# Input gain moved from the projection weights to the rows of x, weight blocks split in pieces of 1024 columns, two pools widened

## The chip, the cores and the metric

The kernel runs as one program on one core of a Trainium2 chip. The metric is the device time of one execution in microseconds (us), the median of several runs. Five engines are meant below: PE (matrix products, with its weight loads shown as PEld), DVE, ACT, POOL, and SP, which here issues every DMA. Each engine takes its instructions in order; semaphores tie the engines together.

## What is computed

Two layers (DEPTH = 2) over 2048 tokens of 1024 float32 features. In each:

```python
h = rmsnorm(x, pre_g)                       # y * pre_g, over the 1024 features
P = h @ W_in                                # 1024 x 2816, columns: u, v, g_A, q, k, v_B, g_B
y_A = u * (W_s @ layernorm(v) + b) * silu(g_A)     # in chunks of 128 tokens, 8 groups of 64
y_B = attention(rope(rmsnorm(q)), rope(rmsnorm(k)), v_B) * silu(g_B)   # 8 query heads, 2 kv heads
x = x + rmsnorm(concat(y_A, y_B) @ W_out, post_g)
```

`pre_g` is a vector of 1024 numbers for each layer. It multiplies the columns of the normalised x, and so can equally multiply the rows of `W_in`.

## The kernel before

**Stages.** A layer is a projection stage and an attention stage. The trace has them at about 0 to 633 us and 633 to 1380 us for layer 0, then to 2011 and 2750 us for layer 1. The projection goes in two halves of two groups; a group (GRP) is 512 tokens.

**Normalised x.** `hT_jobs` gives the jobs of a group. `prep` loads a row tile `x_t` (128 tokens x 1024), lets ACT square it, computes the reciprocal root on DVE with eight tiny operations, and scales it on DVE (L294, two operations of 512 columns) by the row's factor and a constant. `trans` turns it with PE and splits it into a high and a low part, `hT`. The first two groups of layer 1 are scaled in the attention of layer 0 instead (`scale`, L982, tile `x_r`), stored to `h_d`, and read back as `x_h`.

**Weights.** `W_in` is worked off in blocks of 1024 x 256, held as 128 x 8 x 256: one `w_raw` (1 MB, 8 KB a partition), from which `split_w` makes `w_hi` (rounded, ACT, L263) and `w_lo` (the rest, DVE, L264). A product is three passes over them, high x high, high x low, low x high. In `split_w` both operations also multiply by the gain `g_pre`, a pointer to one number per partition; since the gain differs between the eight slices of 128 rows, there are 8 + 8 operations of 256 columns a block. A half has eleven blocks, called here in their order K (keys and values), Q, Q2, VA, VA2, GB, GB2, and four of gates, G0 to G3. The block after the one in use is loaded and split while PE works on the one in use.

**Buffers.** `w_raw`, `w_hi`, `w_lo` and some tiles of the attention share pool `wp`, six buffers of 8 KB a partition. Small work tiles (`fa`, `fb`, `fc`, `fh`, `fl`, `x_h`) share pool `fp`, ten buffers of 2 KB. A tile is given a buffer in program order, and its first writer waits until the last reader of the buffer's former tile is done.

**Order.** Instructions written with `PE`, `ACT`, `DVE`, `POOL` in capitals keep their program order. Those written with `nc.` are placed among them by a scheduler that goes by the tiles' dependences and when buffers become free. So a change of buffers also changes the order on the engines. `bg` is a list of small jobs (transposes, spatial weights) of which the projection does one or two between its passes. `at(k, f)` does the same at step k of the attention. Layer 1's `begin` (block K) is called there, three steps after the end of layer 0's attention.

Of the kernel before, what the change touches and what calls it, by code (L numbers as in the profile page):

```python
# [9 lines left out]
F32 = mybir.dt.float32  # L10
# [3 lines left out]
AF = mybir.ActivationFunctionType  # L14
ALU = mybir.AluOpType
# [4 lines left out]
P = 128  # L20
D = 1024
ND = D // P
GRP = 512
# [6 lines left out]
C_U, C_VA, C_GA, C_Q, C_K, C_GB = 0, 512, 1024, 1536, 2048, 2304  # L30
# [4 lines left out]
NORM_SCALE = -8192.0 / D ** 0.5  # L35
# [3 lines left out]
def encoder(ctx: ExitStack, tc, x, w_in, w_out, pre_g, post_g, ln_a_g, ln_a_b,  # L39
            spatial_w, spatial_b, q_norm_g, k_norm_g, rope, out):  # L40
    nc = tc.nc
# [6 lines left out]

    const = ctx.enter_context(tc.tile_pool(name="const", bufs=1))
    big = ctx.enter_context(tc.tile_pool(name="big", bufs=6))  # L50
    wp = ctx.enter_context(tc.tile_pool(name="wp", bufs=6))
    fp = ctx.enter_context(tc.tile_pool(name="fp", bufs=10))
    rowp = ctx.enter_context(tc.tile_pool(name="rowp", bufs=5))
    lay = ctx.enter_context(tc.tile_pool(name="lay", bufs=1))
    small = ctx.enter_context(tc.tile_pool(name="small", bufs=2))
# [3 lines left out]
    def big_t(shape, name, dt=F32R):  # L59
        return big.tile(shape, dt, name=name, tag="big")  # L60

    def w_t(shape, name, dt=F32R):
        return wp.tile(shape, dt, name=name, tag="w")

    def f_t(name, n=GRP, dt=F32):
        return fp.tile([P, n], dt, name=name, tag="f")

    def row_t(name, shape=(P, D), dt=F32):
        return rowp.tile(list(shape), dt, name=name, tag="row")

    def ps_t(name):
        return psum.tile([P, GRP], F32, name=name, tag="ps", bufs=7)

    class Pinned:


        def __init__(self, engine):
            self.engine = engine
# [8 lines left out]
    PE, ACT, DVE, POOL = Pinned(nc.tensor), Pinned(nc.scalar), Pinned(nc.vector), Pinned(nc.gpsimd)  # L87
# [23 lines left out]
    def x_src(l, t):  # L111
        return x[0, t * P:(t + 1) * P, :] if l == 0 else xn_d[l - 1][t]
# [15 lines left out]
    def rsqrt_row_steps(ss, z, tag, v):  # L128


        m = small.tile([P, 1], F32, name="rs_m", tag=f"rs_m{tag}")
        t = small.tile([P, 1], F32, name="rs_t", tag=f"rs_t{tag}")
        steps = [lambda: v.tensor_scalar(m, ss[:, 0:1], ss[:, 1:2], D * EPS, ALU.add, ALU.add),
                 lambda: v.tensor_scalar(z.bitcast(I32), m.bitcast(I32), -0.5, RSQRT_MAGIC, ALU.mult, ALU.add)]
        for c in (-3.0, -12.0, -768.0):
            steps += [lambda: v.tensor_scalar(t, z, z, m, ALU.mult, ALU.mult),
                      lambda c=c: v.tensor_scalar(z, t, c, z, ALU.add, ALU.mult)]
        return steps
# [36 lines left out]
    class Project:  # L175
        def __init__(self, l):
            self.l = l
            self.stores = []

        def begin(self):  # L180

            self.g_pre = lay.tile([P, ND], F32, name="g_pre", bufs=2)
            raw = self.load_w([C_K])
            nc.sync.dma_start(self.g_pre, pre_g[self.l].rearrange("(t p) -> p t", p=P))
            self.w_kv = self.split_w(raw)

        def gains(self):
            l = self.l
# [65 lines left out]
                                  w_in[self.l, :, c:c + n].rearrange("(d p) e -> p d e", p=P))  # L254
            return raw

        def split_w(self, raw):

            hi = w_t([P, ND, WB], "w_hi")
            lo = w_t([P, ND, WB], "w_lo")  # L260
            for d in range(ND):
                g = self.g_pre[:, d:d + 1]
                nc.scalar.activation(hi[:, d], raw[:, d], AF.Copy, scale=g)  # L263
                nc.vector.scalar_tensor_tensor(lo[:, d], raw[:, d], g, hi.bitcast(F32)[:, d],  # L264
                                               ALU.mult, ALU.subtract)
            return hi, lo

        def hT_jobs(self, g, tail=False):

            hT = [big_t([P, 2, ND // 2, GRP], "hT") for _ in range(2)]  # L270
            xs = [None] * TPG
            act, dve = (ACT, DVE) if tail else (nc.scalar, nc.vector)

            def prep(j):
                def f():
                    done = self.l > 0 and g < HN
                    src = h_d[g * TPG + j] if done else x_src(self.l, g * TPG + j)
                    if done:
                        xs[j] = xt = [f_t("x_h") for _ in range(2)]
                        for i in range(2):  # L280
                            nc.sync.dma_start(xt[i], src[:, i * GRP:(i + 1) * GRP])
                        return
                    row = row_t("x_t")
                    xs[j] = xt = [row[:, 0:GRP], row[:, GRP:D]]
                    nc.sync.dma_start(row, src)
                    junk = ps_t("sq")
                    parts = small.tile([P, 2], F32, name="ss_x", bufs=4)
                    for i in range(2):
                        nc.scalar.activation(junk, xt[i], AF.Square, accum_out=parts[:, i:i + 1])
                    z = small.tile([P, 1], F32, name="rs_x", bufs=4)  # L290
                    for f in rsqrt_row_steps(parts, z, "x", nc.vector):
                        f()
                    for i in range(2):
                        nc.vector.tensor_scalar(xt[i], xt[i], z, 1.0 / NORM_SCALE, ALU.mult, ALU.mult)  # L294
                return f

            def trans(j, q):
                def f():
                    ps = ps_t("pt").rearrange("p (d t) -> p d t", d=4)
                    for d in range(4):  # L300
                        PE.transpose(ps[:, d, :], xs[j][q][:, d * P:(d + 1) * P], ident)
                    sl = slice(j * P, (j + 1) * P)
                    act.copy(hT[q][:, 0, :, sl], ps)
                    dve.tensor_tensor(hT[q][:, 1, :, sl], ps, hT[q].bitcast(F32)[:, 0, :, sl], ALU.subtract)  # L304
                return f
            return hT, [prep(j) for j in range(TPG)], [trans(j, q) for j in range(TPG) for q in range(2)]
# [316 lines left out]
    def attend(l, kv, nxt):  # L623
# [25 lines left out]
        def at(k, f):  # L649
            later.setdefault(k, []).append(f)  # L650
# [298 lines left out]
        def post_steps(s, t, last=False):  # L949
            z = small.tile([P, 1], F32, name="rs_o", bufs=4)  # L950

            def gain(i):
                sl = slice(i * WB, (i + 1) * WB)
                return lambda: POOL.tensor_tensor(s.o[:, sl], s.o[:, sl], g_post[:, sl], ALU.mult)

            def add(hf):
                def f():
                    sl = slice(hf * GRP, (hf + 1) * GRP)
                    DVE.scalar_tensor_tensor(s.o[:, sl], s.o[:, sl], z, s.x[:, sl], ALU.mult, ALU.add)
                    if last and nxt is None:  # L960
                        nc.sync.dma_start(x_dst(l, t)[:, sl], s.o[:, sl])
                return f

            steps = ([gain(i) for i in range(D // WB)] if last else []) + rsqrt_row_steps(s.ss, z, "o", DVE) + [add(0), add(1)]
            def store():
                nc.sync.dma_start(x_dst(l, t), s.o)

            if not last:
                steps.append(store)
            elif nxt is not None:  # L970
                nxt.stores.append(store)
            if nxt is not None and t < HN * TPG:
                ss = small.tile([P, 2], F32, name="ss_o", bufs=4)
                zh = small.tile([P, 1], F32, name="rs_o", bufs=4)

                def square(hf):
                    sl = slice(hf * GRP, (hf + 1) * GRP)
                    return lambda: ACT.activation(s.x[:, sl], s.o[:, sl], AF.Square, accum_out=ss[:, hf:hf + 1])

                def scale(hf):  # L980
                    sl = slice(hf * GRP, (hf + 1) * GRP)
                    return lambda: DVE.tensor_scalar(s.x[:, sl], s.o[:, sl], zh, 1.0 / NORM_SCALE,  # L982
                                                     ALU.mult, ALU.mult)

                steps += [square(0), square(1)] + rsqrt_row_steps(ss, zh, "o", DVE) + [scale(0), scale(1)]
                steps.append(lambda: nc.sync.dma_start(h_d[t], s.x))
            return steps
# [91 lines left out]

        load, last = last_steps()  # L1080
        if nxt is not None:
            at(end + 3, nxt.begin)
        at(total - LAST_0 - 7, load)
        at(total - LAST_0, begin_last)
        for k in range(end + 4):
            if k < total:
                u, i = k // NT, k % NT
                s = state[u]
# [25 lines left out]
            if 0 <= kb < total:  # L1114
                u, i = kb // NT, kb % NT
                s = state[u]
# [5 lines left out]
            if 0 <= kb < total:  # L1122
                u, i = kb // NT, kb % NT
                s = state[u]
# [25 lines left out]
        n = 0  # L1150
# [74 lines left out]
```

## Time and profile before

| | us |
|---|---|
| median of 3 runs (lowest, highest) | 2789.05 (2789.04, 2790.42) |
| the profiled execution | 2785.91 |
| its span in the trace | 2784.1 |
| mean granted clock of PE | 0.994 |
| PE busy | 2681.2 (96%) |
| DVE busy | 1928.6 (69%) |
| ACT busy | 1576.0 (57%) |
| POOL busy | 1279.2 (46%) |
| 352 copies to `w_hi` on ACT, sum | 150.7 |

Busy time is the time in which an engine has an instruction under way; the span runs from the first instruction to the last. About 1.8 us of an execution lie outside the span. The rows of the trace name a line, an engine, an operation, and the tile written and those read.

### The profile page before, as it was taken

How to read it: one execution, taken by the hardware profiler on the slowest of the kernel's cores; microseconds unless marked ns; L12 is line 12 of the kernel's file. 1: busy time of each engine (PE TensorE's matmuls, PEld its weight loads, DVE VectorE, ACT ScalarE, POOL GpSimd, SP SyncE). 2: the span in 40 equal slices, each digit the busy share in tenths (PEclk: the TensorE clock that was granted, in tenths of full speed). 3: DMA queues.
4: the chain of work that ended last, by engine and by line, in shares of the span. 5: the costliest groups of instructions: out<-in, count | busy, mean ns of one | idle time of the engine just before them, and what ended most of it. 6: DMA issues, size and time to landing. Idle time of an engine off the chain costs nothing.

```text
span 2784.1 us, 49014 instructions
## 1 busy us (share of the span) xinstructions
PE 2681.2 (96%) x18230; PEld 1781.7 (64%) x18230; DVE 1928.6 (69%) x4056; ACT 1576.0 (57%) x3263; POOL 1279.2 (46%) x1080
## 2 busy tenths in 40 slices
PE   7999999999999999999999999999999999999997
PEld 7898889764444444444598989897644454444444
DVE  7873797886666766666497638888766666666664
ACT  5322432127887787777642225322288877777774
POOL 1210121007786676767532001210187867767765
PEclk9999999999999999999999999999999999999999
DMA  4433422322222222223344334223222222221313
GB/s 125 142 102 119 144 76 75 115 70 85 87 70 75 85 91 82 81 72 95 126 149 135 118 111 147 73 88 107 84 76 72 74 78 69 75 84 47 104 59 130
DMA packets 277107, 264.31 MB, mean 95 GB/s; under 512 B 21250, under 2 KB 235394, under 8 KB 276868
## 3 DMA queue, kind: packets, MB, share of 16 engines
q1 hardware_dynamic: 276868, 261.18, 29.8%
q8 instruction: 143, 2.34, 0.4%
q14 instruction: 96, 0.79, 0.1%
HBM read 176.05 MB, written 85.07 MB: 94 GB/s over the span
## 4 chain that ended last, share of the span: by engine, by line
PE 75%; DVE 14%; ACT 5%; issue 2%; DMA 2%; SPq 0%; POOL 0%; DVEq 0%; ACTq 0%; POOLq 0%
PE pp L84 26%; PE sp L84 14%; PE pout L84 11%; PE po L84 11%; PE pmax L84 7%; PE sums L84 4%; PE pt L84 2%; DVE w_lo L264 2%; DVE fc L357 2%; ACT p_parts L84 2%; ACT p_f L84 2%; DVE mx L677 1%; DVE fb L442 1%; DMA w_raw<-in_w_in_dram 1%; DVE o_t L84 1%
## 5 line engine op out<-in xcount | busy, mean ns | idle before, releaser
L84 POOL TENSOR_TENSOR p_parts<-p_f,p_parts 128x512 f16<-128x512 f32 x872 | 1032.9, 1203 | 404.2 <-ACT p_f L84 301.7
L84 ACT ACTIVATE p_parts<-sp 128x512 f16<-128x512 f32 x1024 | 628.8, 614 | 293.8 <-PE sp L84 287.3
L84 DVE TENSOR_REDUCE mx<-pmax 128x1 f32<-128x512 f32 x768 | 512.9, 681 | 210.4 <-PE pmax L84 208.5
L84 PE MATMUL pout<-wo,y_t 128*128 128x512 f32 x1488 | 656.1, 505 | 0.6 <-ACT p_f L84 0.3
L84 PE MATMUL po<-p_parts,v_st 128*32 128x512 f16 (+1 forms) x3072 | 638.0, 383 | 0.2
L84 ACT ACTIVATE p_f<-sp 128x512 f32<-128x512 f32 x1024 | 630.0, 615 | 0.0
L84 PE MATMUL pp<-w_hi,hT 128*128 128x256 f32 x3584 | 502.7, 289 | 14.8 <-DVE hT L304 10.1
L84 PEld LDWEIGHTS pp<-w_hi,hT 128*128 128x128 f32 x3584 | 462.2, 194 | 24.6 <-DVE hT L304 10.7
L84 PE MATMUL pmax<-k_t,q_m 128*128 128x512 f16 x1024 | 389.3, 382 | 10.7 <-DVE mx L677 3.3
L84 PE MATMUL sp<-q_st,k_t 128*128 128x512 f16 x1024 | 389.5, 380 | 7.3 <-DVE mx L84 4.6
L84 PEld LDWEIGHTS <-v_st 128*32 128x32 f16 (+1 forms) x3072 | 193.2, 96 | 309.2 <-issue 252.1
L84 PE MATMUL sp<-q,k_t 66*128 66x512 f16 x1024 | 390.4, 381 | 0.0
L84 PEld LDWEIGHTS pout<-wo,y_t 128*128 128x128 f32 x1488 | 280.8, 190 | 128.3 <-issue 9.2
L84 PEld LDWEIGHTS <-k_t 128*128 128x128 f16 (+1 forms) x2048 | 191.4, 99 | 186.6 <-issue 73.2
L462 POOL TENSOR_TENSOR fl<-fa,fh 128x512 fp32r<-128x512 f32 x32 | 42.1, 1317 | 518.6 <-ACT fh L461 430.4
L84 PE MATMUL pp<-hT,w_hi 128*128 128x512 f32 x1024 | 271.7, 413 | 0.0
L84 PE MATMUL pp<-w_lo,hT 128*128 128x256 f32 x1792 | 264.0, 288 | 5.7 <-DVE w_lo L264 5.5
L263 ACT ACTIVATE w_hi<-w_raw,g_pre 128x256 fp32r<-128x256 f32 x352 | 150.7, 499 | 171.8 <-DMA w_raw<-in_w_in_dram 111.1
L84 PE MATMUL sums<-p_parts,one_h 128*32 128x512 f16 x2048 | 242.1, 380 | 0.0
L84 PEld LDWEIGHTS pp<-w_lo,hT 128*128 128x128 f32 x1792 | 233.8, 192 | 10.8 <-DVE w_lo L264 9.3
L84 PEld LDWEIGHTS pp<-hT,w_hi 128*128 128x128 f32 x1024 | 193.2, 189 | 35.4
L677 DVE TENSOR_REDUCE mx<-pmax 128x1 f32<-128x512 f32 x256 | 173.0, 686 | 37.0 <-PE pmax L84 35.3
(160 smaller groups left out, 2839.9 us busy)
## 6 DMA issues: line engine op xcount, KB each, us to landing
w_raw<-in_w_in_dram SPq DMA_DIRECT2D x28, 1024.0 KB
y_t<-y_d SPq DMA_DIRECT2D x56, 512.0 KB
w_raw<-in_w_in_dram SPq DMA_DIRECT2D x32, 512.0 KB
x_t<-in_x_dram SPq DMA_DIRECT2D x16, 512.0 KB
z_d<-fb SPq DMA_DIRECT2D x32, 256.0 KB
gb_d<-fa SPq DMA_DIRECT2D x32, 256.0 KB
fb<-z_d SPq DMA_DIRECT2D x32, 256.0 KB
y_d<-fh SPq DMA_DIRECT2D x32, 256.0 KB
```

Source lines behind the costliest of these rows:

```text
L84: return tc.keep_in_program_order(call(*args, **kw))
L263: nc.scalar.activation(hi[:, d], raw[:, d], AF.Copy, scale=g)
L264: nc.vector.scalar_tensor_tensor(lo[:, d], raw[:, d], g, hi.bitcast(F32)[:, d], ALU.mult, ALU.subtract)
L357: nc.vector.tensor_tensor(t2[:, :, :, lo:lo + 16], qn[:, :, :, hi:hi + 16], tbi[:, :, 1:2, lo:lo + 16].broadcast_to([P, 2, n, 16]), ALU.mult)
L442: nc.vector.scalar_tensor_tensor(s.zt[r, c, :], pz[r, h * P:(h + 1) * P], self.lng[r, c:c + 1], self.zbias[r, c, :], ALU.mult, ALU.add)
L462: nc.gpsimd.tensor_tensor(lo, th, hi.bitcast(F32), ALU.subtract)
L677: dve.tensor_reduce(s.mx[:, j, c:c + 1], ps, AX.X, ALU.max)
```

## The change

The gain is no longer applied in `split_w`. A new function `norm_row` loads `pre_g` of a layer as one row, copied to all 128 partitions (`g_row`, 128 x 1024, 512 KB written), and ACT multiplies it by the constant. The scale of `x_t` and that of `x_r` then multiply by the row's factor and by `g_row`. `split_w` makes plain copies and plain subtractions of four slices, 1024 columns; for the K block in `begin`, of two. The load of `g_pre` is gone. `wp` gets a seventh buffer, `fp` twelve instead of ten.

```diff
-    wp = ctx.enter_context(tc.tile_pool(name="wp", bufs=6))
-    fp = ctx.enter_context(tc.tile_pool(name="fp", bufs=10))
+    wp = ctx.enter_context(tc.tile_pool(name="wp", bufs=7))
+    fp = ctx.enter_context(tc.tile_pool(name="fp", bufs=12))
...
+        def norm_row(self):
+            self.g_row = lay.tile([P, D], F32, name="g_row")
+            nc.sync.dma_start(self.g_row, pre_g[self.l].partition_broadcast(P))
+            nc.scalar.mul(self.g_row, self.g_row, 1.0 / NORM_SCALE)
...
         def begin(self):
-            self.g_pre = lay.tile([P, ND], F32, name="g_pre", bufs=2)
-            raw = self.load_w([C_K])
-            nc.sync.dma_start(self.g_pre, pre_g[self.l].rearrange("(t p) -> p t", p=P))
-            self.w_kv = self.split_w(raw)
+            self.w_kv = self.split_w(self.load_w([C_K]), 2)
...
-        def split_w(self, raw):
+        def split_w(self, raw, n=4):
             hi = w_t([P, ND, WB], "w_hi")
             lo = w_t([P, ND, WB], "w_lo")
-            for d in range(ND):
-                g = self.g_pre[:, d:d + 1]
-                nc.scalar.activation(hi[:, d], raw[:, d], AF.Copy, scale=g)
-                nc.vector.scalar_tensor_tensor(lo[:, d], raw[:, d], g, hi.bitcast(F32)[:, d],
-                                               ALU.mult, ALU.subtract)
+            for d in range(0, ND, n):
+                sl = slice(d, d + n)
+                nc.scalar.copy(hi[:, sl], raw[:, sl])
+                nc.vector.tensor_tensor(lo[:, sl], raw[:, sl], hi.bitcast(F32)[:, sl], ALU.subtract)
...
                     nc.sync.dma_start(row, src)
+                    if self.g_row is None:
+                        self.norm_row()
...
-                        nc.vector.tensor_scalar(xt[i], xt[i], z, 1.0 / NORM_SCALE, ALU.mult, ALU.mult)
+                        nc.vector.scalar_tensor_tensor(xt[i], xt[i], z, self.g_row[:, i * GRP:(i + 1) * GRP],
+                                                       ALU.mult, ALU.mult)
...
-                    return lambda: DVE.tensor_scalar(s.x[:, sl], s.o[:, sl], zh, 1.0 / NORM_SCALE,
-                                                     ALU.mult, ALU.mult)
+                    return lambda: DVE.scalar_tensor_tensor(s.x[:, sl], s.o[:, sl], zh, nxt.g_row[:, sl],
+                                                            ALU.mult, ALU.mult)
...
         if nxt is not None:
+            at(1, nxt.norm_row)
             at(end + 3, nxt.begin)
```

The change also moves instructions. SP in layer 0's first half, where the loads of Q2, VA and VA2 are issued (`w_raw_768`, `w_raw_952` and, two rows below the end, VA2's). Before:

```order
L253 DMA w_raw_768<-in_w_in_dram 128x8x256
L214 DMA lng_1126<-in_ln_a_g_dram 128x4x1
L184 DMA g_pre_16244<-in_pre_g_dram 128x8x1
L238 DMA sb_row_1140<-in_spatial_b_dram 1x1024
L334 DMA fa_725<-in_rope_dram 128x4x128
L334 DMA fa_885<-in_rope_dram 128x4x128
L253 DMA w_raw_952<-in_w_in_dram 128x8x256
L409 DMA q_d0_112<-fh_997 64x2x256 x2
L409 DMA q_d0_112<-fl_998 64x2x256 x2
L409 DMA q_d0_112<-fh_1026 64x2x256 x2
L409 DMA q_d0_112<-fl_1027 64x2x256 x2
```

After the change (`w_raw_749` is Q2, `w_raw_921` VA, `w_raw_1465` VA2):

```order
L257 DMA w_raw_749<-in_w_in_dram 128x8x256
L218 DMA lng_1095<-in_ln_a_g_dram 128x4x1
L242 DMA sb_row_1109<-in_spatial_b_dram 1x1024
L257 DMA w_raw_921<-in_w_in_dram 128x8x256
L340 DMA fa_706<-in_rope_dram 128x4x128
L340 DMA fa_866<-in_rope_dram 128x4x128
L257 DMA w_raw_1465<-in_w_in_dram 128x8x256
L415 DMA q_d0_112<-fh_966 64x2x256 x2
L415 DMA q_d0_112<-fl_967 64x2x256 x2
L415 DMA q_d0_112<-fh_995 64x2x256 x2
L415 DMA q_d0_112<-fl_996 64x2x256 x2
```

VA's load now stands ahead of two loads of rope rows, and VA2's ahead of the eight stores of q.

DVE in layer 0's second half, among the rope work of the queries (`fc`, `fl`, `ms_q`). Before, the block split here is VA:

```order
L357 TENSOR_TENSOR fc<-fc,fa 128x2x2x16 x4
L359 TENSOR_TENSOR fc<-fc 128x2x128
L264 SCALAR_TENSOR_TENSOR w_lo<-w_raw,g_pre,w_hi 128x256 x4
L405 TENSOR_TENSOR fl<-pt,fh 128x512 x2
L264 SCALAR_TENSOR_TENSOR w_lo<-w_raw,g_pre,w_hi 128x256 x4
L345 TENSOR_REDUCE ms_q<-fb 128x8 x2
```

After it, it is VA2:

```order
L363 TENSOR_TENSOR fc<-fc,fa 128x2x2x16 x4
L365 TENSOR_TENSOR fc<-fc 128x2x128
L268 TENSOR_TENSOR w_lo<-w_raw,w_hi 128x1024
L411 TENSOR_TENSOR fl<-pt,fh 128x512
L268 TENSOR_TENSOR w_lo<-w_raw,w_hi 128x1024
L411 TENSOR_TENSOR fl<-pt,fh 128x512
L351 TENSOR_REDUCE ms_q<-fb 128x8 x2
```

The same kind of place now holds the block that comes one later in the program.

DVE at the boundary of the layers, where the last sums (`den`, from which PE's `pd` is made) stand beside layer 1's K block. Before:

```order
L84 TENSOR_TENSOR o_t_16110<-pout_16145,o_t_16110 128x512
L264 SCALAR_TENSOR_TENSOR w_lo_16249<-w_raw_16245,g_pre_16244,w_hi_16248 128x256 x3
L84 STREAM_TRANSPOSE den_16190<-sums_144 128x512
L264 SCALAR_TENSOR_TENSOR w_lo_16249<-w_raw_16245,g_pre_16244,w_hi_16248 128x256
L84 RECIPROCAL rden_16202<-pd_16192 128x4
```

After it:

```order
L268 TENSOR_TENSOR w_lo_15991<-w_raw_15988,w_hi_15990 128x512 x4
L84 TENSOR_TENSOR o_t_15854<-pout_15889,o_t_15854 128x512
L84 STREAM_TRANSPOSE den_15934<-sums_144 128x512
L84 RECIPROCAL rden_15946<-pd_15936 128x4
L84 TENSOR_TENSOR gb_15339<-gb_15339,rden_15946 128x4x64
```

The whole K block is now split ahead of `den`. Some fifteen and twenty rows further on, the two `w_lo` of block Q stand ahead of the MEMSET of `k_t` and of the first `hT` of layer 1; before, all of block Q came behind both. On SP the load of that block stood between the first eight and the last eight loads of `x_h`, and now stands ahead of all sixteen.

More of the change, by code (lines that the diff above doesn't have):

```diff
@@ L178, in __init__ @@
             self.stores = []
+            self.g_row = None
+        def norm_row(self):
+            self.g_row = lay.tile([P, D], F32, name="g_row")
+            nc.sync.dma_start(self.g_row, pre_g[self.l].partition_broadcast(P))
+            nc.scalar.mul(self.g_row, self.g_row, 1.0 / NORM_SCALE)
         def begin(self):
-            self.g_pre = lay.tile([P, ND], F32, name="g_pre", bufs=2)
-            raw = self.load_w([C_K])
-            nc.sync.dma_start(self.g_pre, pre_g[self.l].rearrange("(t p) -> p t", p=P))
-            self.w_kv = self.split_w(raw)
+            self.w_kv = self.split_w(self.load_w([C_K]), 2)
         def gains(self):
```

## The prediction

> **What bounds the kernel now.** I read the page's busy line and its chain first, then busy time by stretch, then the tile `w_raw`, then the timelines of the stretches that stood out.
>
> ```profile
> PE 2681.2 (96%) x18230; PEld 1781.7 (64%) x18230; DVE 1928.6 (69%) x4056; ACT 1576.0 (57%) x3263; POOL 1279.2 (46%) x1080
> PE 75%; DVE 14%; ACT 5%; issue 2%; DMA 2%; SPq 0%; POOL 0%; DVEq 0%; ACTq 0%; POOLq 0%
> ```
>
> PE is busy 2681.2 of 2784.1 us, and the change takes no matmul away: the most that any edit of the other engines could give back is the 103 us in which PE has no work. DVE holds 14% of the chain, so some of those gaps are DVE's. Where they lie, by stretch (columns: length, then PE, PEld, DVE, ACT and POOL busy with counts, PE's granted clock, DMA share, GB/s):
>
> ```profile
> 0.00:40.00 40.00, 20.82 (x130) 20.07 (x130) 26.58 (x89) 24.27 (x62) 1.97 (x7) 0.91 0.61 195
> 80.00:130.00 50.00, 45.20 (x329) 40.88 (x329) 44.96 (x111) 17.06 (x40) 15.62 (x11) 0.97 0.48 148
> 300.00:345.00 45.00, 43.32 (x318) 40.69 (x317) 39.19 (x132) 27.58 (x68) 6.92 (x6) 1.00 0.49 159
> 345.00:412.00 67.00, 61.26 (x483) 59.23 (x483) 61.84 (x161) 17.11 (x42) 16.65 (x13) 0.97 0.27 81
> 460.00:520.00 60.00, 56.40 (x423) 51.70 (x423) 57.69 (x125) 16.39 (x35) 5.34 (x4) 1.00 0.34 100
> 620.00:1380.00 760.00, 743.51 (x5033) 355.55 (x5032) 499.59 (x896) 597.78 (x1202) 539.90 (x453) 1.00 0.26 83
> 1380.00:1412.00 32.00, 25.33 (x165) 20.66 (x164) 24.96 (x51) 17.17 (x42) 12.43 (x17) 0.95 0.78 272
> 1470.00:1510.00 40.00, 35.79 (x266) 31.88 (x266) 38.60 (x87) 14.36 (x32) 14.37 (x10) 1.00 0.49 152
> 1724.00:1791.00 67.00, 61.04 (x481) 59.02 (x481) 61.52 (x154) 17.37 (x43) 16.93 (x13) 0.97 0.27 79
> ```
>
> In the attention stretch (620 to 1380) PE is 98% busy and no weights are split; nothing is to be won there. In 80 to 130, 345 to 412, 1470 to 1510 and 1724 to 1791, which are the projection stretches with the rope work, DVE is as busy as PE or nearly, and PE stands idle 4.8, 5.7, 4.2 and 6.0 us, 20.7 us together. That is the prize this change can reach. The tile view of `w_raw` says who is late there:
>
> ```profile
> L263 ACT ACTIVATE w_hi<-w_raw,g_pre x352: 491/495/567, 8.2 to 1943.1; 128x256 fp32r<-128x256 f32 x176
> L264 DVE SCALAR_TENSOR_TENSOR w_lo<-w_raw,g_pre,w_hi x352: 444/477/1575, 8.7 to 1967.5; 128x256 fp32r<-128x256 f32 x176
>   DMA w_raw<-in_w_in_dram: 111.1, 25
>   DVE w_lo L264: 47.4, 12
> ```
>
> (us waited, times.) ACT stands 111.1 us at 25 copies of weights until the raw block has landed, and 47.4 us at twelve until DVE has finished with an older block. ACT itself has time; what is queued behind those copies on its in-order queue has not.
>
> **Two parts of the change.** One is cheaper splitting: 44 blocks (11 per half, 2 halves, 2 layers), each now 8 + 8 operations of 256 columns. The other is the seventh buffer of the pool that holds `w_raw`, `w_hi` and `w_lo`. With six, two split blocks (four tiles), one raw block and one `w_hi` fill it, so the next `w_lo` and the next raw load wait for the block in use. The order of instructions shows the effect of seven: nearly every split stands one block earlier on DVE, and the raw loads one block earlier on SP (in layer 0's first half VA2's load moves ahead of the eight `q_d` stores).
>
> Price of the split. Nothing of 1024 columns in this form stands in the trace, so I take the nearest rows:
>
> ```profile
> L642 DVE TENSOR_TENSOR wo<-wo_raw,wo x16: 678/682/1787, 623.1 to 2007.0; 128x512 fp32r<-128x512 f32 x16
> L1014 ACT ACTIVATE g_post<-g_post x2: 1058/1060/1063, 335.7 to 1714.2; 128x1024 f32<-128x1024 f32 x2
> 360.95 2.27 DVE L480 TENSOR_REDUCE v_top<-v_st 128x1 f32<-128x2048 f32 x1
> 1385.33 1.27 DVE L264 SCALAR_TENSOR_TENSOR w_lo<-w_raw,g_pre,w_hi 128x256 fp32r<-128x256 f32 x3 [1.56 <-ACT w_hi L263]
> ```
>
> On DVE 512 columns cost 0.682 and 2048 (another operation) 2.27, so 1.03 ns a column, and 1024 columns about 0.682 + 512 x 1.03 ns = 1.21. Eight at 0.477 are 3.82 us, two at 1.21 are 2.42: 1.4 us a block by durations. In a run of equal operations they overlap a little (the last row: three in 1.27 us, so 0.42 each), and 8 x 0.42 = 3.4 against 2.4 is **about 1 us a block**, which I use; 1.4 is the upper end, and 0 the lower, should a pair of wide operations lose to POOL what it saves. On ACT 8 x 0.495 = 4.0 becomes 2 x 1.06 = 2.1; ACT waits for data here, so this is worth nothing in itself except that a block is ready 1 to 2 us earlier.
>
> **First halves (80 to 130, 1470 to 1510).**
>
> ```profile
> 80.00:130.00 50.00, 8.92 (x16) 0.97 0.48 148
> 345.00:412.00 67.00, 10.10 (x24) 0.97 0.27 81
> 88.05 0.47 SPq L253 DMA_DIRECT2D w_raw<-in_w_in_dram  x1
> 91.96 2.00 DVE L357 TENSOR_TENSOR fc<-fc,fa 128x128 f32<-128x128 f32 x4 [1.36 <-POOL fa L336]
> 94.54 2.11 ACT L263 ACTIVATE w_hi<-w_raw,g_pre 128x256 fp32r<-128x256 f32 x5 [10.27 <-DMA w_raw<-in_w_in_dram]
> 102.21 1.22 PE L84 MATMUL pp<-w_hi,hT 128*128 128x256 f32 x8 [1.01 <-DVE k_t L390]
> ```
>
> (The first two rows are stretches for line 264 alone: 16 `w_lo` operations, two blocks, 8.92 us, and 24 in 10.10. In the others: start, length; in brackets the idle time before and what ended it.) The load of VA2 issues at 88.05 and lands 6.5 us later; ACT waits 10.27 us for it in front of everything else. Two blocks at 8.92 become 2 x 2.4 = 4.8, which is 4.1 us off a DVE that has 5.0 us spare, beside a PE with 4.8 us of gaps. Part of the 8.92 moves to other stretches since the blocks move; I take **-4 us each, -8 together**, range 0 to -10.
>
> **Second halves (345 to 412, 1724 to 1791).**
>
> ```profile
> 378.31 1.28 DVE L345 TENSOR_REDUCE ms_q<-fb 128x8 f32<-128x512 f32 x2 [3.11 <-ACT fb L344]
> 387.18 0.66 PE L84 MATMUL pt<-ident,fc 128*128 128x128 f32 x4 [1.98 <-DVE fc L359]
> 391.10 0.66 PE L84 MATMUL pt<-ident,fc 128*128 128x128 f32 x4 [1.37 <-DVE fc L359]
> 402.91 2.76 PE L84 MATMUL pp<-w_lo,hT 128*128 128x256 f32 x7 [1.12 <-DVE w_lo L264]
> 406.86 0.48 PE L84 MATMUL pp<-w_lo,hT 128*128 128x256 f32 x1 [1.20 <-DVE w_lo L264]
> 412.14 1.71 ACT L263 ACTIVATE w_hi<-w_raw,g_pre 128x256 fp32r<-128x256 f32 x4 [9.60 <-DMA w_raw<-in_w_in_dram]
> ```
>
> DVE idles 3.11 us because ACT's `fb` stands behind a copy of weights; DVE's rope product `fc` is then late, and PE waits 1.98 and 1.37 for it. Later PE waits 1.12 and 1.20 for VA2's `w_lo`. With the split one block earlier the last two waits have no reason, and the 3.11 us go with ACT's wait. The three blocks of 10.10 us become 3 x 2.4 = 7.3, 2.8 us of DVE beside that. The four waits make 5.7 us, PE's whole idle time there. Two things hide in its busy time. The seven matmuls after 402.91 take 394 ns each where this group's mean is 288 (row below), 0.7 us. And the stretch's clock is 0.97 where 460 to 520 has 1.00; that is up to 3% of 61 us, 1.8 us, if it has to do with the gaps, which I count in part. I take **-7 each, -14 together**, range -3 to -16.
>
> ```profile
> L84 PE MATMUL pp<-w_lo,hT 128*128 128x256 f32 x1792 | 264.0, 288 | 5.7 <-DVE w_lo L264 5.5
> ```
>
> **460 to 520 and its like in layer 1:** DVE is 57.69 of 60 us busy, and the rope is over; PE idles 3.6. Two blocks save 2 us of DVE, but the reduces of `pmax` bind there; I take -1 each, **-2**, range 0 to -4.
>
> **What the change adds.** The scale of x by a constant and a row factor becomes a product with a row of gains:
>
> ```profile
> L294 DVE TENSOR_SCALAR x_t<-x_t,rs_x x48: 473/480/1543, 10.5 to 1708.2; 128x512 f32<-128x512 f32 x48
> L84 DVE SCALAR_TENSOR_TENSOR o_t<-o_t,rs_o,x_r x48: 737/1288/1773, 873.3 to 2742.1; 128x512 f32<-128x512 f32 x48
> ```
>
> Undisturbed, 480 becomes 737, 0.26 each: 48 make 12.3 us of DVE, 16 of them in each of three preparations; 16 more in the attention stretch cost 4 us where DVE has 260 us to spare, so nothing. Sixteen cost 4.1; in 300 to 345 DVE is 39.19 of 45 us busy, so 5.8 are free, and PE idles only 1.7; I count a quarter: **+1 each there and in its like in layer 1, +2**, range 0 to +8. Against this stands the median of that same row, 1288 ns: in the attention, beside POOL, such an operation takes 0.55 us longer. The Trainium skill gives a reason in "SBUF — State Buffer", section "Who interferes with whom": a DVE instruction with two SBUF inputs and a GpSimd instruction that reads SBUF hold each other off for the whole instruction. [...] By that rule each of the 16 operations that meets POOL would be 0.55 dearer, 8.8 us if all do; POOL is busy 6.92 of those 45 us, so an estimate by the rule is 15% of that, 1.3 us, with which the sum would be about one or two us higher.
>
> **Start.** The gains now come as a broadcast row of 512 KB and an ACT multiply of 1.06 us, in the place of `g_pre`.
>
> ```profile
> 8.15 3.30 ACT L263 ACTIVATE w_hi<-w_raw,g_pre 128x256 fp32r<-128x256 f32 x8 [2.16 <-DMA g_pre<-in_pre_g_dram]
> 29.50 3.78 PE L84 MATMUL pp<-w_hi,hT 128*128 128x256 f32 x16 [6.70 <-DVE hT L304]
> ```
>
> `w_hi` no longer waits 2.16 us for `g_pre`. The row stands ahead of the other x tiles: 512 KB at the stretch's 195 GB/s are 2.7 us, which is the upper end for the later x tiles, on which `hT` and so PE's 29.50 depend. The order puts ACT's multiply between the two squares of the first tile, 1.06 later for all behind. Between a gain of 2.16 and a loss of 2.7 + 1.06 I take **+0.5**, range -2 to +4.
>
> **Boundary between the layers (1380 to 1412).**
>
> ```profile
> 1384.74 2.10 ACT L263 ACTIVATE w_hi<-w_raw,g_pre 128x256 fp32r<-128x256 f32 x5 [6.55 <-DMA w_raw<-in_w_in_dram]
> 1387.38 0.24 PE L84 MATMUL pd<-den,two_v 128*32 128x4 f32 x8 [2.27 <-DVE den L84]
> 1403.13 3.47 DVE L1180 MEMSET k_t<- 2x4096 f16 x1 [0.91 <-issue]
> 1407.38 1.11 PE L84 MATMUL pt<-ident,x_h 128*128 128x128 f32 x4 [4.40 <-DVE hT L84]
> ```
>
> The order now puts all four `w_lo` of C_K (4 x 0.68 = 2.7) ahead of the last `den`; three of eight (1.27) stood there. If C_K lands no earlier, `den` is 1.4 later; but its load is now ahead of the rows and `a_d` loads on SP, so I take +0.5 of it. C_Q's two `w_lo` (2 x 1.21 = 2.4) now stand ahead of the MEMSET behind which `hT`, and PE's 4.40 us wait at 1407.38, are queued: +2.4 if they have their data, more if C_Q is late. One is among adds that DVE has slack for. **+2.5** in all, range 0 to +6.
>
> **Sum:** -8 - 14 - 2 + 2 + 0.5 + 2.5 = **-19 us**. The profiled execution took 2785.91 (1.8 more than its span); 2785.91 - 19 = 2766.9. The median of the runs is 3.1 above the profiled execution, so I say **2770**.
>
> **Rivals.**
>
> *DVE stays the bound (no change).* If DVE's rope and reduce work sets the pace in the four stretches whatever the splits do, then only the time of the splits comes off, and where one stretch's last wait is `fc` behind `pt` the DVE time is not on PE's path. For it: DVE's 44.96 of 50 and 38.60 of 40 us. Against it: 3.11 us idle at 378.31. First halves -2, second halves -4, pmax -1, boundary +4, start +2, prep +2: +1, so 2790.
>
> *The split in front (slower).* DVE is in order, and the split now stands one block earlier. If the raw block lands no earlier than before, the waits that are ACT's (10.27, 9.60, and by the likeness of the rows 1470 and 1724 the same again in layer 1, 40 us in all) become waits of DVE ahead of rope work that PE needs. DVE spare in those four stretches is 5.0 + 5.2 + 1.4 + 5.5 = 17 us; beyond it 23 us land on PE, with the +5 of the additions 28: 2817. It decides where a raw load issues less than about 6.5 us (88.05 to 94.54) before DVE comes to its `w_lo`. Against it: the loads move earlier on SP by the same one block, as far as their consumers do.
>
> *More comes back.* If the splits were the cause of nearly every gap, PE's idle time in the four stretches (20.7), 3 each of the pmax stretches, and a share of the 19 us of the start would go: -32, so 2757.
>
> **How the numbers follow.** The forecast (2758 to 2783) 0.70, more 0.08, no change 0.13, slower 0.09. 0.2% of the time, 5.6 us, is about what a measurement of this kernel can tell from no change: faster is below 2783.5, slower above 2794.6. The range 2750 to 2788 leaves out the slower case, and the upper half of the no-change case; at the low end it holds what both upper ends of the two big terms give (-26) with something from the start. Faster 0.78, same 0.13, slower 0.09.
>
> **What the changed profile would show.** 84 copies and 84 subtractions of 1024 columns near 1.06 and 1.21 us, 8 of 512; the wait of ACT for `w_raw` far under 111 us in sum; no wait of PE for `w_lo` near 400; DVE busy some 28 us lower (44 off the splits, 16 onto the scales); x scales at 737 or near it, and long ones only beside POOL; PE's idle time in the four stretches half or less; the boundary slightly worse. It is wrong if DVE shows new waits for `w_hi` or the `w_raw` DMA, if x scales lie near 1288 in the preparation, or if PE's gaps in 345 to 412 remain though the splits came early.

## The result, and the profile after

The changed kernel takes 2773.3 us (median of 4 runs, 2771.47 to 2776.35) against 2789.05 (4 runs, 2788.07 to 2790.42): a ratio of 0.9944, 95% interval 0.9932 to 0.9957, 15.7 us less. The forecast was 2770. Its profiled execution took 2771.47 us, 14.4 less than that of before, with a span of 2769.3.

The page's busy line and chain, after:

```profile
PE 2677.1 (97%) x18230; PEld 1782.0 (64%) x18230; DVE 1896.8 (68%) x3796; ACT 1522.7 (55%) x3005; POOL 1287.0 (46%) x1080
PE 77%; DVE 11%; ACT 5%; DMA 3%; issue 2%; POOL 1%; SPq 0%; DVEq 0%; POOLq 0%; ACTq 0%
```

DVE has 31.8 us less to do and 11% of the chain instead of 14%. The same stretches as before (everything sits some microseconds earlier or later in them; columns as there):

```profile
80.00:130.00 50.00, 44.91 (x333) 41.23 (x333) 43.55 (x100) 14.69 (x27) 16.22 (x12) 0.97 0.49 150
345.00:412.00 67.00, 64.00 (x524) 63.55 (x524) 60.33 (x143) 20.04 (x41) 16.02 (x13) 0.97 0.23 67
460.00:520.00 60.00, 59.22 (x457) 55.44 (x455) 55.50 (x112) 14.53 (x23) 6.11 (x4) 1.00 0.41 124
1470.00:1510.00 40.00, 37.95 (x296) 35.10 (x295) 35.41 (x82) 9.93 (x17) 12.78 (x9) 1.00 0.49 150
1724.00:1791.00 67.00, 66.44 (x558) 66.09 (x557) 61.76 (x140) 20.38 (x39) 18.97 (x14) 1.00 0.27 80
```

PE's idle time in the four rope stretches is 5.1, 3.0, 2.1 and 0.6 us, together 10.7 where it was 20.7; the first did not improve. The tile view of `w_raw`, after (durations as minimum/median/maximum ns, then us waited and times):

```profile
L267 ACT CAST w_hi<-w_raw x92: 613/1047/1058, 9.9 to 1913.7; 128x1024 fp32r<-128x1024 f32 x84, 128x512 fp32r<-128x512 f32 x8
L268 DVE TENSOR_TENSOR w_lo<-w_raw,w_hi x92: 680/1218/2103, 10.5 to 1921.4; 128x1024 fp32r<-128x1024 f32 x84, 128x512 fp32r<-128x512 f32 x8
  PE pp L84: 100.3, 31
  DMA w_raw<-in_w_in_dram: 38.4, 8
  ACT w_hi L267: 25.7, 15
```

ACT's wait for landing weights fell from 111.1 to 38.4 us, and its 47.4 us behind DVE are gone. What holds a split now is mostly PE (100.3 us, before 23.7): the buffer is still being read, and PE is at work meanwhile.

**A ledger by matmul.** PE executes the same 18230 matmuls in the same order in both traces. So the start of the n-th matmul in the trace of before can be subtracted from its start in the changed kernel's, and the change of that difference along the span says where time was lost (+) or won (-), in us:

| stretch (time before) | predicted | measured |
|---|---|---|
| start, to 60 | +0.5 | +1.6 |
| first half, layer 0 (60 to 140) | -4 | -0.4 |
| preparation of x (300 to 345) | +1 | +2.6 |
| second half, layer 0 (345 to 460) | -7 | -4.3 |
| 460 to 520 | -1 | -4.3 |
| attention, layer 0 (520 to 1380) | 0 | +1.8 |
| boundary (1380 to 1430) | +2.5 | +1.4 |
| first half, layer 1 (1470 to 1520) | -4 | -3.5 |
| preparation (1680 to 1724) | +1 | +1.9 |
| second half, layer 1 (1724 to 1840) | -7 | -9.1 |
| 1840 to 1900 | -1 | -3.6 |
| all else | 0 | +0.9 |
| sum | -19 | -15.0 |

It rests on one execution of each kernel. The runs of one kernel spread over up to 8.5 us (E1 below), so single entries are good to a microsecond or two.

**PE's clock in the ledger.** Part of that spread can be seen. The granted clock of PE falls to half for 3.4 us, or for two or three times that, at six places of the trace of before and at seven of the changed kernel (the end of the span aside). Three stretches, of before, of the changed kernel, and of E4 below at the same place as the second (columns as above; the third from the end is the granted clock):

```profile
407.00:410.40 3.40, 3.40 (x17) 3.40 (x18) 3.06 (x11) 0.00 (x0) 1.27 (x1) 0.50 1.05 344
1693.30:1696.70 3.40, 3.40 (x18) 3.40 (x18) 3.40 (x17) 2.72 (x9) 0.00 (x0) 0.50 0.92 306
1691.00:1697.00 6.00, 6.00 (x53) 6.00 (x52) 6.00 (x23) 4.17 (x15) 1.17 (x2) 1.00 0.94 305
```

Where PE has work all through, 3.4 us at half clock cost half of it, 1.7 us; the ledgers show steps of 1.5 to 1.6. In the 14 traces of this case there are 84 such places, and each follows at least 1.2 us of idle PE within the 3.4 us before it. The converse does not hold: the same wait of 1.9 us, near 1150 us, is followed by half clock in ten of the traces and by full clock in four. So a wait of PE can cost 1.7 us more than its length in one execution and not in another, and an entry of about that size need not belong to an edit.

Three waits stand behind entries that missed. First, layer 1's row of gains at 333 us (start, length, engine, and in brackets the idle time before and what ended it):

```profile
321.75 0.38 SPq L257 DMA_DIRECT2D w_raw<-in_w_in_dram  x1
332.84 0.34 SPq L184 DMA_DIRECT2D g_row<-in_pre_g_dram  x1
331.41 1.40 DVE L299 SCALAR_TENSOR_TENSOR x_t<-x_t,rs_x,g_row 128x512 f32<-128x512 f32 x2
336.91 1.06 ACT L185 ACTIVATE g_row<-g_row 128x1024 f32<-128x1024 f32 x1 [6.23 <-DMA g_row<-in_pre_g_dram]
```

`g_row` has one buffer. The load for layer 1 was placed at the earliest point at which the program allows it, right behind the last scale of x in layer 0. SP's queue then stood from 322 to 333 for the buffer, and ACT, in order, 6.23 us for the landing, with the `fb` and `hT` copies of layer 0 behind it in the queue.

Second, in layer 0's first half, two equal operations of DVE, what POOL did at the second, and the wait of PE behind it:

```profile
120.67 0.17 DVE L125 SCALAR_TENSOR_TENSOR rs_y<-rs_t,rs_y 128x16 f32<-128x16 f32 x1
...
121.50 1.26 DVE L125 SCALAR_TENSOR_TENSOR rs_y<-rs_t,rs_y 128x16 f32<-128x16 f32 x1
121.48 1.26 POOL L342 TENSOR_TENSOR fa<-fa,gain_q 128x512 f32<-128x512 f32 x1 [6.09 <-issue]
123.23 2.05 PE L84 MATMUL pp<-w_hi,hT 128*128 128x256 f32 x8 [2.47 <-DVE zbias L250]
```

Third, in the second half, where the forecast had the waits for `fc` vanish:

```profile
384.59 0.55 SPq L340 DMA_DIRECT2D fa<-in_rope_dram  x1
387.72 1.30 POOL L342 TENSOR_TENSOR fa<-fa,gain_q 128x512 f32<-128x512 f32 x1 [10.70 <-DMA fa<-in_rope_dram]
389.05 1.96 DVE L363 TENSOR_TENSOR fc<-fc,fa 128x128 f32<-128x128 f32 x4 [2.57 <-POOL fa L342]
PE pt L84 <- DVE fc L365: 3.0, 1, 3.0
```

(The last row is PE's waits from 380 to 400: us, times, longest.) ACT's `fb` is no longer late there, but the rope rows are: their load issues at 384.59, behind eight stores of q on SP, POOL waits for it, DVE for POOL, PE for DVE.

### The profile page after: what moved, and what is told of

Same layout as the page of the kernel before. It is cut to its first block, busy times and chain, and to the rows that moved or that the text cites. A ratio compares the mean times of both kernels' runs of the same rounds, so it can differ in the third digit from the quotient of the medians.

```text
span 2769.3 us, 48428 instructions
## 1 busy us (share of the span) xinstructions
PE 2677.1 (97%) x18230; PEld 1782.0 (64%) x18230; DVE 1896.8 (68%) x3796; ACT 1522.7 (55%) x3005; POOL 1287.0 (46%) x1080
## 4 chain that ended last, share of the span: by engine, by line
PE 77%; DVE 11%; ACT 5%; DMA 3%; issue 2%; POOL 1%; SPq 0%; DVEq 0%; POOLq 0%; ACTq 0%
PE pp L84 27%; PE sp L84 14%; PE po L84 11%; PE pout L84 11%; PE pmax L84 7%; PE sums L84 4%; PE pt L84 2%; DVE fc L363 2%; ACT p_parts L84 2%; ACT p_f L84 2%; DMA w_raw<-in_w_in_dram 1%; DVE mx L84 1%; DVE o_t L84 1%; DVE w_lo L268 1%; ACT w_hi L267 1%
## 5 line engine op out<-in xcount | busy, mean ns | idle before, releaser
L84 PEld LDWEIGHTS <-q_m 128*128 128x128 f16 x1024 | 99.8, 98 | 140.2 <-issue 42.1
```

Source lines behind the costliest of these rows:

```text
L84: return tc.keep_in_program_order(call(*args, **kw))
```

## The experiments

Theory A: the seventh large buffer is the gain, since it brings loads and splits one block forward. Theory B: the gain is DVE's saving from fewer, wider pieces. All medians stand against 2789.05 to 2789.8 us of the kernel before, measured with each set of experiments; E9 to E12 ran on another chip than E1 to E8; the kernel before took 2789.79 us there.

**E1, the pools alone.**

```diff
-    wp = ctx.enter_context(tc.tile_pool(name="wp", bufs=6))
-    fp = ctx.enter_context(tc.tile_pool(name="fp", bufs=10))
+    wp = ctx.enter_context(tc.tile_pool(name="wp", bufs=7))
+    fp = ctx.enter_context(tc.tile_pool(name="fp", bufs=12))
```

> The kernel before with only the two pools widened (7 and 12 buffers); splits of 256 columns with the gain stay. Theory A (the seventh buffer brings each load and split one block forward, and that is the gain): about 2776, some 13 us under the kernel before, and nothing of the losses at the preparations of x; the matmuls of 400 to 420 come 4 to 6 us earlier. Theory B (fewer microseconds of DVE in the splits are the gain): within 3 us of before, 2786 to 2790.

2775.16 us, ratio 0.9944 (0.9928 to 0.9960): the whole gain without the rest of the change. The median is A's. By the ledger the matmuls up to 410 came 5.9 us earlier, as A said, but in the next 10 us another wait took 8.6 us, so that those at 420 came 2.7 us later. DVE and PE there:

```profile
417.40 0.28 DVE L209 TENSOR_SCALAR gain_q<-gain_q,g_exp 128x128 f32<-128x128 f32 x1 [9.88 <-DMA gain_q<-in_q_norm_g_dram]
419.75 1.12 PE L84 MATMUL pt<-ident,fc 128*128 128x128 f32 x4 [7.97 <-DVE fc L359]
```

Layer 1's `gain_q`, a tile of one buffer like `g_row`, is prefetched here; its load (issued at 408.0) waited for layer 0's last use, and its first operation stands on DVE ahead of layer 0's rope.

**E2, the rest without the pools.**

```diff
-    wp = ctx.enter_context(tc.tile_pool(name="wp", bufs=7))
-    fp = ctx.enter_context(tc.tile_pool(name="fp", bufs=12))
+    wp = ctx.enter_context(tc.tile_pool(name="wp", bufs=6))
+    fp = ctx.enter_context(tc.tile_pool(name="fp", bufs=10))
```

> The changed kernel with the pools as they were (6 and 10 buffers). Theory A (buffers): no better than before, 2787 to 2795, since ACT waits for the raw blocks as it did (about 110 us) and the dearer scale of x and the boundary cost 6 us. Theory B (cheaper splits): 2773 to 2778, as the whole change.

2797.32 us, ratio 1.0027 (1.0017 to 1.0036): slower than before, and above what A expected. Its wait for landing weights, and its row of gains:

```profile
  DMA w_raw<-in_w_in_dram: 130.2, 28
339.87 1.06 ACT L185 ACTIVATE g_row<-g_row 128x1024 f32<-128x1024 f32 x1 [9.10 <-DMA g_row<-in_pre_g_dram]
```

DVE does 28.3 us less than before (1900.3 against 1928.6 busy), and the kernel is slower: B falls.

**E3, ten small buffers instead of twelve**, the changed kernel otherwise.

> The changed kernel with ten small work buffers instead of twelve, seven large ones kept. Both theories of the large buffers and of the splits give the whole gain without the two small ones: 2772 to 2775. If the small buffers matter (rope rows loaded earlier, fewer waits at fc and fb), 2778 or more.

2773.81 us (2773.16 to 2774.86), ratio 0.9943 (0.9927 to 0.9960). The small buffers do nothing measurable.

**E4, layer 1's row of gains at a fixed place in the attention.**

```diff
-            at(1, nxt.norm_row)
+            at(1, nxt.norm_row_load)
+            at(24, nxt.norm_row_scale)
```

The two new functions are the two halves of `norm_row`: the load, kept in program order, and ACT's multiply.

> The changed kernel with layer 1's row of gains loaded and multiplied within the attention of layer 0 at a fixed place, instead of at 333 us where its load stood in SP's queue until the last x_t of layer 0 was scaled, and ACT's multiply waited 6.2 us for it. If that wait is what costs 2.1 us at 340, it goes: 2 us under the changed kernel, 2771, and the matmuls from 345 on come 2 us earlier. If the dearer scale of x is the cost there, nothing moves.

2770.06 us, ratio 0.9929 (0.9914 to 0.9944), 3.2 under the changed kernel; their runs overlap (2767.12 to 2773.43 against 2771.47 to 2776.35), so the times alone do not show it. The ledger's step from 300 to 345 is +0.45 instead of +2.60. So 2.1 us of the preparation's 2.6 were this wait. The row now loads beside other work:

```profile
L190 SPq DMA_DIRECT2D g_row<-in_pre_g_dram x1: 630/630/630, 629.9 to 629.9; - x1
L84 ACT ACTIVATE g_row<-g_row x1: 1069/1069/1069, 656.7 to 656.7; 128x1024 f32<-128x1024 f32 x1
```

**E5, E1 with two buffers for `gain_q` and `gain_k`.**

```diff
-            self.gain_q = lay.tile([P, 2, HD], F32, name="gain_q")
-            self.gain_k = lay.tile([P, 2, HD], F32, name="gain_k")
+            self.gain_q = lay.tile([P, 2, HD], F32, name="gain_q", bufs=2)
+            self.gain_k = lay.tile([P, 2, HD], F32, name="gain_k", bufs=2)
```

> The kernel before with the wide pools of the first experiment, and two buffers instead of one for the small rope gains gain_k and gain_q, so that layer 1's need not wait for layer 0's last use. In the first experiment DVE stood 9.88 us at 407.5 for the load of layer 1's gain_q, and PE 8.0 us for the rope product behind it. If that wait is an accident of where a prefetch was placed, it goes: 2765 to 2769, under the changed kernel, without moving the gain and without wide pieces. If the stretch is bound by DVE's work, the wait turns up elsewhere and the time stays 2773 to 2777.

2763.34 us, ratio 0.9907 (0.9889 to 0.9925), a little better than expected: 11.8 under E1 and 10.0 under the changed kernel, with the gain in the weights and pieces of 256. The ledger's step from 400 to 420 is now -6.05, to the hundredth what the changed kernel has there. Free of the accident, the buffers alone are worth 25.7 us. (The kernel before with the two `gain` buffers only was not run; in its trace no operation waits for the landing of `gain_q`.)

**E6, the changed kernel with pieces of 256 columns.**

```diff
-            self.w_kv = self.split_w(self.load_w([C_K]), 2)
+            self.w_kv = self.split_w(self.load_w([C_K]), 1)
...
-        def split_w(self, raw, n=4):
+        def split_w(self, raw, n=1):
```

> The changed kernel, but with the weights split in eight pieces of 256 columns as before (plain copies and subtractions, no gain). Theory A (the seventh buffer is the gain, the width is worth some microseconds in the stretches where DVE is full): 2775 to 2781. Theory B (width is the gain): 2785 or more.

2785.69 us, ratio 0.9988 (0.9978 to 0.9997): B's number, which seemed to make the width worth 12.4 us. But the order had moved again, and E1's accident was back:

```profile
423.44 0.28 DVE L213 TENSOR_SCALAR gain_q<-gain_q,g_exp 128x128 f32<-128x128 f32 x1 [10.56 <-DMA gain_q<-in_q_norm_g_dram]
```

**E9, E6 with E5's two buffers** (and eleven small ones, for room).

> The sixth experiment (changed kernel, pieces of 256 columns) with two buffers for gain_k and gain_q, paid for by one of the twelve small work buffers. There DVE stood 10.56 us at 413 for layer 1's gain_q and PE 8.0 us behind it. If most of the 12 us by which the narrow pieces trail the changed kernel are this one wait, and not the width: 2776 to 2779. If the width itself is worth 12 us: 2784 or more.

2774.03 us, ratio 0.9943 (0.9927 to 0.9959), 11.7 under E6 and 0.7 from the changed kernel. In the sum the width is worth nothing that can be measured; E9 also has two buffers for each gain, for which E12 below leaves up to 2.9 us open. At single places it does count. By the ledgers of all kernels, in us against before:

| stretch (time before) | 256 columns, 7 buffers (E1, E5, E6, E9) | 1024, 7 (changed, E3, E4) | 1024, 6 (E2, E11) |
|---|---|---|---|
| 460 to 520 and 1840 to 1900 | -3.4 to -5.4 | -7.0 to -7.9 | -3.7, -3.9 |
| boundary (1380 to 1430) | -1.0 to -1.2 | +1.4 to +1.8 | +2.1, +2.5 |

Wide pieces win some 3 us in the stretches of the `pmax` reduces, with and without the buffer, and lose about as much at the boundary of the layers, where with seven buffers they stand on DVE ahead of a MEMSET (see E8).

E5 and E9 differ in where the gain is applied (and by one small buffer, which E3 makes idle): moving it to the rows of x costs 10.7 us in this setting. The largest entry is the wait for the row, 8.13 us of ACT in E9: from 300 to 345 its ledger has +6.3, that of E5 -0.3.

**E7, the scale of x as before** (gain left out).

```diff
-  nc.vector.scalar_tensor_tensor(xt[i], xt[i], z, self.g_row[:, i * GRP:(i + 1) * GRP], ALU.mult, ALU.mult)
+  nc.vector.tensor_scalar(xt[i], xt[i], z, 1.0 / NORM_SCALE, ALU.mult, ALU.mult)
```

and the same at `x_r`.

> The changed kernel with the rows of x scaled by a constant as before, so the input gain is left out of the computation; the row of gains is still loaded and multiplied. It prices the dearer scale, 64 operations. If it costs what the prediction took (0.26 us each of DVE, a quarter of it on the path in the preparations, nothing in the attention): 2769 to 2772, some 2 us under the changed kernel. If it also makes the 1.7 us that layer 0's attention lost: 2767 to 2769. If it costs nothing: 2773.

2767.26 us, ratio 0.9922 (0.9906 to 0.9938), 6.0 under the changed kernel. Not all of it is the scale: nothing reads the row here, so its buffer is free early and E4's wait goes too (300 to 345: +0.45). From 1000 to 1380 the ledger has -0.01 instead of +1.30: the dearer `x_r` does cost that in the attention. (E3, E4, E6, E8 and E11, with the dearer scale, have +1.25 to +1.35; E5 and E10, with the old one, -0.03 and +0.01. E2, E9 and E12 with the dearer scale and E1 with the old one are about 1.6 lower: they lack the half clock near 1150.) In the preparation at 1680 to 1724 it has +1.92, as the changed kernel (+1.93): that entry is not the scale. Nor is the largest step of the 6.0 us, -4.2 instead of -0.4 in layer 0's first half, where the changed kernel met the 1.26 us operation and half clock behind it. So 6.0 us is not the price of the scale.

**E11, E2 with the row as in E4.**

> The second experiment (changed kernel with six and ten buffers) with layer 1's row of gains loaded in the attention, as in the fourth. The second experiment lost 5.3 us at 345, where ACT waited 9.1 us for that row. Without it, 2791 to 2793: still not faster than before, if without the seventh buffer the wide pieces have nothing to save. If the row was all that hid a gain of the pieces: 2786 or less.

2792.61 us, ratio 1.0010 (1.0001 to 1.0020): 4.7 under E2, as expected, and still not faster than before. Without the seventh buffer the rest of the change saves nothing in the sum: what the wide pieces win from 460 to 520 and from 1840 to 1900 (-3.9) is lost in the two preparations of x (+3.4 and +3.6).

**E8, E4 with the MEMSET of `k_t` on POOL.**

```diff
-        nc.vector.memset(kv[1][HD:HD + 2], 1.0)
+        nc.gpsimd.memset(kv[1][HD:HD + 2], 1.0)
```

> The fourth experiment's kernel (row of gains of layer 1 loaded in the attention) with the MEMSET of k_t on POOL instead of DVE. At 22 and 1402 us the 3.47 us of this MEMSET stand on DVE ahead of hT, for which PE waits 4.6 and 4.5 us, and the wide w_lo of block Q stand ahead of it. If the queue on DVE makes those waits, each falls by 2 to 3.5 us: 2763 to 2766. If the transposes' data (x) are late anyway, nothing: 2770.

2760.76 us, ratio 0.9899 (0.9883 to 0.9914), 9.3 under E4 and more than expected. POOL does it early, and PE's waits for `hT`, 4.74 and 4.50 us in E4, shrink to 2.86 and 0.55, by 5.8 us together. The half clock of PE that E4 shows at both places (0.83 on average from 20 to 40 and from 1390 to 1410 us) is gone as well (1.00 from 20 to 40 and from 1385 to 1410), which can explain the excess. The rows of E8:

```profile
1.38 3.50 POOL L1197 MEMSET k_t<- 2x4096 f16 x1
28.04 1.69 PE L84 MATMUL pp<-w_hi,hT 128*128 128x256 f32 x12 [2.86 <-DVE hT L319]
1394.30 0.66 PE L84 MATMUL pt<-ident,x_h 128*128 128x128 f32 x4 [0.55 <-DVE hT L84]
```

**E10, E5 with E8's MEMSET; E12, E8 with E5's two buffers** (and eleven small ones).

> The fifth experiment (gain still in the weights, pieces of 256, wide pools, two buffers for gain_k and gain_q) with the MEMSET of k_t on POOL. By the eighth experiment's ledger the MEMSET costs about 5 us at the start, and at the boundary 3.5, which is its own length (the other 3 there came from block Q's pieces ahead of it, which this kernel lacks): 2754 to 2756. If the two do not add: 2760 or more.

> The eighth experiment with two buffers for gain_k and gain_q and eleven small work buffers. In that kernel DVE waits only 0.2 us for layer 1's gain_q, so there is nothing to take away: 2759 to 2762. If it is under 2757, the prefetch cost something there that the waits do not show.

E10: 2758.63 us, ratio 0.9885 (0.9867 to 0.9902), 4.7 under E5 where 7 to 9 were expected. E12: 2757.89 us, ratio 0.9883 (0.9868 to 0.9898), 2.9 under E8 where nothing was, and between its two cases; the intervals of E8 and E12 overlap, so this stays undecided. Their traces differ in PE's clock: half at six places in E8 and at one in E12, though both have the waits of 1.9 us near 948 and 1142. Both beat the changed kernel, by 14.7 and 15.4 us. With the accidents and the MEMSET out of the way, the two forms of the gain and of the split are 0.7 us apart, no difference. The MEMSET cost 9.3 us with wide pieces (E8) and 4.7 with narrow ones (E10); it does not explain the 10.7 us of E9 over E5, since both have narrow pieces and the same ledger at the boundary (-1.2 and -1.0). Beyond the wait for the row, these 10.7 us stay open. All medians:

| gain, pieces | 6 large buffers | 7 | 7, two `gain` buffers | 7, also the MEMSET on POOL |
|---|---|---|---|---|
| weights, 256 | 2789.1 | 2775.2 (E1) | 2763.3 (E5) | 2758.6 (E10, two `gain` buffers) |
| rows, 256 | - | 2785.7 (E6) | 2774.0 (E9) | - |
| rows, 1024 | 2797.3 (E2) | 2773.3 (changed) | - | - |
| rows, 1024, row in the attention | 2792.6 (E11) | 2770.1 (E4) | - | 2760.8 (E8), 2757.9 (E12, two `gain` buffers) |

## Why the prediction was right, and where its steps were not

The time and its sign came out, and of the two mechanisms that were named, the seventh buffer is shown (E1, E5 against E2, E11). The attribution inside the sum was partly wrong, and that the sum came so near is in part luck: first halves +4.1, preparation +2.5 and attention +1.8 above the forecast, 460 to 520 and its like 5.9 below it, cancel for the most part.

- **Price of the split: right; its worth: wrong.** 1218 and 1047 ns were measured for 1.21 and 1.06 us, and DVE's busy time fell by 31.8 us where 28 was said. But the 1 us a block of DVE, on which parts of the -8, -14 and -2 rested, buys nothing measurable in the sum (E9 against the changed kernel), nor without the buffer (E2, E11). Where it did count was in the stretches from 460 and 1840 us, for which the least was forecast.
- **First halves: -8, measured -3.9.** Layer 1 gave -3.5. In layer 0 PE waits 2.47 us for `zbias`, at the end of a string of tiny DVE operations of which one took 1.26 us instead of some 0.17; half clock follows, from 123.1 to 126.5. Without that long operation E7 and E12 wait 1.38 and 1.40 us there. E3, E4 and E8, with the same buffers and pieces, have -2.5, -1.8 and 0.0 in layer 0, so the -0.4 is one draw of several.
- **Second halves: -14, measured -13.4, by other waits than named.** "The 3.11 us go with ACT's wait" failed: they became 2.57 for POOL's `fa`, and the `fc` waits of 1.98 and 1.37 became one of 3.0. What came back were the matmuls of 400 to 420 (-6.05); in the changed trace PE waits for `w_lo` nowhere. Of these 6.05, 2.3 are the two waits named. The half clock of before from 407.0 to 410.4 is up to 1.7, near the 1.8 that the prediction counted in part. The seven matmuls at 402.91 lost 1.7, not 0.7: matmuls overlap, so the price of one is not its mean duration of 288 ns, but 264.0 us over 1792, 147 ns.
- **460 to 520 and its like: -2, measured -7.9,** outside the stated 0 to -4. PE idles 0.8 of the 60 us instead of 3.6. Both halves of the change are in it: E5, with the buffers and pieces of 256, has -3.3 and -2.1 in the two layers; E2, with wide pieces and six buffers, -1.7 and -2.1. The splits stayed in the stretch and got cheaper (15 `w_lo` of 7.62 us before, 4 of 4.85 after), so they lay on PE's path here, where the forecast let the reduces bind.
- **Preparation: +2, measured +4.5.** 746 ns for `x_t` (737 forecast) was right, and long ones were rare. The 2.1 us of the row's load (E4) were not forecast at all: the step that counted the row's load at the start only left out the one of layer 1. Of the +1.9 at 1700, 1.5 are PE's clock: half from 1693.3 to 1696.7, behind a wait of 2.13 us. E4 has the same wait, full clock, and +0.43.
- **Attention: 0, measured +1.8 in layer 0.** The scale of `x_r` went from 844 to 1112 ns, and E7 shows 1.3 us of it on PE's path. "DVE has 260 us to spare" is an average; at single steps PE waits for DVE's next operation.
- **Boundary: +2.5, measured +1.4.** `hT` came 2.0 us later (2.4 was said), through block Q's `w_lo` ahead of the MEMSET; E8 shows that this queue on DVE makes PE's wait. Another 0.7 came behind it, with PE at half clock for 6.8 us from 1403.1, where before it was 3.4. `den` came 1.3 us earlier instead of 0.5 later, since its wait fell from 2.27 to 0.97. The rows, after:

```profile
1383.18 0.25 PE L84 MATMUL pd<-den,two_v 128*32 128x4 f32 x8 [0.97 <-DVE den L84]
1396.84 1.25 DVE L268 TENSOR_TENSOR w_lo<-w_raw,w_hi 128x1024 fp32r<-128x1024 f32 x1
1400.88 3.47 DVE L1187 MEMSET k_t<- 2x4096 f16 x1 [0.91 <-issue]
1405.13 1.12 PE L84 MATMUL pt<-ident,x_h 128*128 128x128 f32 x4 [4.49 <-DVE hT L84]
```

- **Rivals.** That the split in front would hand ACT's waits to DVE did happen in part: DVE waits for `w_hi` 25.7 us in 15 places, where before it was 2.6 in 2. The prediction had named such waits as a sign of being wrong; they did not reach PE, which waits for `w_lo` nowhere in the changed kernel (before: 5.5 us in five places). A mechanism of this kind did strike, with a smaller thing in front: a prefetch of gains (E1, E6, 8 us of PE).

## What to carry to other kernels

When an edit bundles a pool's size with cheaper operations, run each half alone: here the wider pools gave all of it, and 32 us of engine time saved bought nothing in the sum, since what they won in one stretch a longer queue lost in another. Where a scheduler places loads as early as buffers allow, look for every tile of one buffer that the next stage prefetches; its load waits for the last use in this stage, and holds an in-order queue and the first operation behind it for up to 10.6 us. Compare two kernels matmul by matmul before crediting a parameter: E6 gave its 12 us to the width, and they belonged to a prefetch. Look at PE's granted clock in the same stretch too, before an entry of 1.5 us is given to an edit.

## What the runs showed of the hardware

A DVE operation on 16 columns, 0.17 us in its equal before it, took 1.26 us when POOL's product of 512 columns had started 0.02 us before it, and both ended within 0.02 us of each other (121.50 and 121.48). The Trainium skill states such a lock in "SBUF — State Buffer", section "Who interferes with whom", for a DVE instruction with two SBUF inputs against a GpSimd instruction that reads SBUF; this pair agrees with it, down to the whole length of POOL's instruction. It is not the only one: the trace of before has seven such operations, of 0.98 to 1.25 us, each ending 0.03 us behind a product of POOL that it ran into. By that rule what it costs depends on the overlap and not on the DVE operation's size, so a string of tiny operations is as exposed as a wide one. The scale of x shows the same dependence on the company it keeps (the last row is of before):

```profile
L299 DVE SCALAR_TENSOR_TENSOR x_t<-x_t,rs_x,g_row x48: 739/746/1786, 11.9 to 1703.4; 128x512 f32<-128x512 f32 x48
L84 DVE SCALAR_TENSOR_TENSOR x_r<-o_t,rs_o,g_row x16: 721/1112/1732, 880.2 to 1227.1; 128x512 f32<-128x512 f32 x16
L84 DVE TENSOR_SCALAR x_r<-o_t,rs_o x16: 473/844/1469, 885.3 to 1230.4; 128x512 f32<-128x512 f32 x16
```

The same operation has a median of 746 ns in the preparations and 1112 in the attention, where POOL is busy 542.52 of 760 us. The old form with one input tile was held up too: 480 ns in the preparations and 844 in the attention. In each kernel twelve of the sixteen `x_r` end a fixed time behind a product of POOL, 0.28 us before and 0.55 after. So the row of gains did not bring this collision; it adds 0.27 us to such an operation, and 0.26 to one that is not held up.
